# Modulation columns of a diffusion backbone: four blocks in one accumulation, transposes in place of selector matmuls

## The chip, the core and the metric

The kernel runs on one core of a Trainium2 chip. The metric is the device time of one execution in microseconds (us). In the profile, PE is TensorE's matmuls and PEld its weight loads, DVE is VectorE, ACT is ScalarE, POOL is GpSimd and SP is SyncE, which here issues DMAs. Each engine takes its instructions in the order in which they stand in the program, and waits for other engines by semaphores.

## What is computed

Two layers over a latent grid of 1024 positions and a context of 256, with a width of 1024: first windowed attention with 16 query heads and 4 key/value heads, then a bidirectional state-space scan. Before each mixer the normalised input is scaled and shifted, and what the mixer gives is multiplied by a gate. Scale, shift and gate come from two condition vectors, one for the latents and one for the context:

```python
def adaln(cond, w, b):
    mod = jax.nn.silu(cond) @ w + b
    return jnp.split(mod, 3, axis=-1)

for i in range(DEPTH):
    shift, scale, gate = adaln(c, w_ada[i], b_ada[i])
    shift_c, scale_c, gate_c = adaln(c_ctx, w_ada[i], b_ada[i])
    u = rms_normalize(h) * (1.0 + scale[:, None]) + shift[:, None]
    uc = rms_normalize(hc) * (1.0 + scale_c) + shift_c
    ...
    h = h + gate[:, None] * y
```

So each layer has a matrix w_ada of 1024 x 3072, by which two vectors are multiplied. The result for the layer is wanted with its 3072 values along the partitions, as 24 tiles of 128, and two columns (latents, context): the array mod.

## The kernel before

The activations lie transposed, features on partitions, in three token tiles: i = 0 and 1 (512 latents each) and i = 2 (256 context positions). Matmuls of the projections are done with operands split into a high and a low part: three fp32r matmuls for each of 8 slices of 128 features (lines L227 to L229, into PSUM tiles named pj), 24 matmuls for a projection of 128 outputs and one token tile. Weights are loaded by SP into tiles wr; ACT casts the high part (wh, L213), POOL or DVE subtracts the low part (wl, L215).

The stage of qkvg computes keys and values first. Then a loop over x = 0..7 computes queries for the token tiles 2 and 0 (q_step), and a second loop over x = 0..7 computes gates (g_step, tile 2 for all x, tile 0 for x from 4 on). Behind each of these projections, fill(m) takes m small steps (3, 3, 3, 2 in turn) off a list named ada. That list is the modulation work that isn't needed at once: of the 12 column blocks of 512 columns (6 for each layer), layer 0's blocks 0 to 3 are done at the start (ada0), and the eight blocks left, (0, 4), (0, 5) and (1, 0) to (1, 5), are fillers.

For a block, adaln_col makes nine steps. Steps k = 0..7 each load one slab of w_ada of 128 x 512 (256 KB) into a buffer of the rings wh or wl, four buffers each. After the fourth and the eighth load, four matmuls run. Each has a stationary operand of 32 columns (the condition vectors at feature slice k, in the first two of 32 columns, the rest zero) and the slab as the moving one, and writes 32 of the 128 PSUM partitions of the tile aps: a strip of TensorE's array for each of four values of k. So the sum over k lies spread over four strips when the block is done. The ninth step, fin, copies aps to SBUF (L189, tile qf), and modulation (L201) multiplies each of its four 128-column parts by a selector sel of 128 x 2 that adds the four strips up and brings the columns onto partitions; DVE adds the bias (L203), and adds 1 or halves where the block is a scale or a layer 0 gate (L205, L192).

The instructions of an engine are not in the order of the code. A scheduler orders them when the program is built, by dependencies, priorities and its own expectation of when things are ready. Behind the stage, the pools of the stage are closed; attention (att_front, att_back) then runs with the rest of the query and gate projections as its own fillers.

Of the kernel before, what the change touches and what calls it, by code (L numbers as in the profile page):

```python
# [9 lines left out]
F32 = mybir.dt.float32  # L10
# [3 lines left out]
ALU = mybir.AluOpType  # L14
# [3 lines left out]
P = 128  # L18
D = 1024
KT = D // P  # L20
# [85 lines left out]
class Kernel:  # L106
# [13 lines left out]
    def t(self, pool, shape, dt, tag, bufs=None):  # L120
        self.n += 1
        kw = {"bufs": bufs or BUFS.get(tag, 1)}
        return pool.tile(shape, dt, tag=tag, name=f"{tag}_{self.n}", **kw)
# [45 lines left out]
        self.bada = t(cp, [P, 2, 24], F32, "bada")  # L169
        nc.sync.dma_start(self.bada, self.a["bada"].rearrange("p (l t) -> p l t", l=2))  # L170

    def adaln_col(self, layer, n, pool, ps):

        nc, t = self.nc, self.t
        st = {}

        def step(k):
            if k == 0:
                st["ps"] = t(ps, [P, 512], F32, "aps", 2)
            raw = t(pool, [P, 4, P], F32, ("wh", "wl")[k // 4])  # L180
            nc.sync.dma_start(raw, self.a["w_ada"][layer, n, k].rearrange("p (a c) -> p a c", a=4))
            st[k] = raw
            if k % 4 == 3:
                for j in range(4):
                    nc.tensor.matmul(st["ps"][32 * j : 32 * j + 32], self.cs[:, k - 3 + j, :], st[k - 3 + j].rearrange("p a c -> p (a c)"), start=k == 3, stop=k == KT - 1)

        def fin():
            row = t(self.pq, [P, 512], F32, "qf")
            nc.scalar.copy(row, st["ps"])  # L189
            m = self.modulation(layer, n, row, ps)  # L190
            if n // 2 == 2 and layer == 0:
                nc.vector.tensor_scalar_mul(m, m, 0.5)  # L192

        return [lambda k=k: step(k) for k in range(KT)] + [fin]

    def modulation(self, layer, n, row, ps):

# [322 lines left out]
    def qkvg(self, p, wk, wvp):  # L520
        nc, t, a = self.nc, self.t, self.a
        ps = self.psA
        nc.gpsimd.dma_start(self.mask, a["mask"])
        nc.sync.dma_start(self.sink, a["sink"].broadcast_to([P, HEADS]))
        nc.vector.tensor_scalar_mul(self.nsink, self.sink, -1.0)
        v = self.v
        NB = (LAT + CTX) // P
        kh_d = [[t(self.dr, [P, n], F32, f"k{x}_{i}") for i, (_, n) in enumerate(TT)] for x in range(2)]

        wv = [self.load_w(a["wv"][q // 2, :, q % 2 * 512 : q % 2 * 512 + 512], 2, 256, pool=wvp, eng=nc.gpsimd) for q in range(4)]  # L530

        def kproj(x, i):
            s, n = TT[i]
            h, l = self.qk(p, self.proj_h(ps, wk[x], self.uH, self.uL, i), i)
            nc.vector.tensor_copy(self.kL[x][:, s : s + n], l)
            nc.sync.dma_start(kh_d[x][i], h.bitcast(F32))
            for e in range(2):
                for hf in range(2):
                    nc.gpsimd.dma_start(self.kHH[2 * x + e][hf * HD : (hf + 1) * HD, s : s + n], kh_d[x][i][e * HD : (e + 1) * HD, :])

        def vproj(b):
            i = 0 if b < 4 else (1 if b < 8 else 2)
            o = (b * P) - TT[i][0]
            pj = t(ps, [P, 512], F32, "pj")
            self.mm3(pj[:, :256], [(self.uH[i][:, k, o : o + P], self.uL[i][:, k, o : o + P],
                                    wv[k // 2][0][:, k % 2, :], wv[k // 2][1][:, k % 2, :]) for k in range(KT)])
            pv = pj[:, :256].rearrange("p (j d) -> p j d", j=KV)
            nc.scalar.copy(v[:, b, :, :HD], pv)
            nc.vector.tensor_sub(v[:, b, :, HD:], pv, v[:, b, :, :HD])  # L549

        for i, (s, n) in enumerate(TT):
            for x in range(2):
                kproj(x, i)
            if not VLAST:
                for b in range(s // P, (s + n) // P):
                    vproj(b)
        for b in range(NB if VLAST else 0):
            vproj(b)
        ada = []
        for layer, n in [(0, 4), (0, 5)] + [(1, n) for n in range(6)]:  # L560
            ada += self.adaln_col(layer, n, wvp, ps)

        def fill(m):
            for f in ada[:m]:
                f()
            del ada[:m]

        n = [3, 3, 3, 2]
        for x in range(8):
            w = self.load_halves(a["wq"][x])  # L570
            for i in (2, 0):
                self.q_step(p, w, x, i)
                fill(n[x % 2 * 2 + (i == 0)])
        for x in range(8):
            w = self.load_halves(a["wg"][x])
            for i in (2, 0) if x >= G0 else (2,):
                self.g_step(p, w, x, i)
                fill(n[x % 2 * 2 + (i == 0)])
        fill(len(ada))
# [972 lines left out]
```

## Time and profile before

| what | us |
|---|---|
| three runs: 1886.82, 1890.34, 1890.7; median | 1890.34 |
| span of the profiled execution, first to last instruction | 1886.0 |
| PE busy in it | 1790.8 (95%) |
| DVE busy | 1186.5 (63%) |
| ACT busy | 906.5 (48%) |
| POOL busy | 751.1 (40%) |

The profile is of one execution, of which only the span is given. The mean granted TensorE clock is 0.979 of full speed. The slices of the page show the rough shape; each digit is a busy share in tenths, for a fortieth (47 us) of the span:

```profile
PE   6779998899999899879999999999999999999997
PEclk9889999999999999989999999999999999999998
DMA  9338765653345456220111111111111111433552
```

The fillers lie in the fourth to sixth slice. A row of the timeline gives start, duration, engine, line, operation, output and inputs, shapes and how many records were merged; idle time before it and what ended it stand in brackets. An fp32 matmul of the fillers shows as two records (x8 is four strips), an fp32r matmul of the projections as one, an fp32 transpose as one. Consecutive matmuls overlap, so the distance from start to start is what one takes, not its duration.

### The profile page before, as it was taken

To read this page: it belongs to the slowest core of one execution; us is meant where nothing else is said; L and a number is where in the kernel's file an instruction comes from. 1 tells how busy PE (TensorE), PEld (TensorE's weight loads), DVE (VectorE), ACT (ScalarE), POOL (GpSimd) and SP (SyncE) were. 2 spreads that over 40 slices of the span, in tenths; PEclk is the share of its full clock that TensorE was granted. 3 is DMA by queue.
4 is the path that set the end of the run, shared out by engine and by line. 5 is a ranking of instruction groups with operands and counts; after the bars stand their busy time and mean duration, and the time that the engine had idled before them with its cause. 6 is when DMAs were issued, how large, how long until landed. Compare 5 with 4: busy or idle time off the path is not lost. (4 is left out here: it accounts for less than half of the span.)

```text
span 1886.0 us, 29647 instructions
## 1 busy us (share of the span) xinstructions
PE 1790.8 (95%) x10632; PEld 1543.2 (82%) x10632; DVE 1186.5 (63%) x2214; ACT 906.5 (48%) x1863; POOL 751.1 (40%) x1026
## 2 busy tenths in 40 slices
PE   6779998899999899879999999999999999999997
PEld 3678776788889787668898898989889898988887
DVE  4753425887777766584665757666575766754743
ACT  4522225677787765472353534434353543543532
POOL 2731105664456464302334352524335252442411
PEclk9889999999999999989999999999999999999998
DMA  9338765653345456220111111111111111433552
GB/s 358 111 79 251 233 209 132 143 124 95 96 118 135 112 137 198 87 55 23 49 36 44 44 36 44 36 44 36 43 47 33 44 39 41 138 119 100 176 162 68
DMA packets 147204, 192.10 MB, mean 102 GB/s; under 512 B 15313, under 2 KB 84817, under 8 KB 147057
## 3 DMA queue, kind: packets, MB, share of 16 engines
q1 hardware_dynamic: 112992, 171.56, 29.1%
q0 software_dynamic: 34064, 18.65, 5.6%
q8 instruction: 84, 1.38, 0.3%
q14 instruction: 64, 0.52, 0.1%
HBM read 154.54 MB, written 35.92 MB: 101 GB/s over the span
## 5 line engine op out<-in xcount | busy, mean ns | idle before, releaser
L227 PE MATMUL pj<-uH,wh 128*128 128x512 f32 (+1 forms) x712 | 258.8, 365 | 27.1 <-DVE v L549 9.5
L228 PE MATMUL pj<-uL,wh 128*128 128x512 f32 (+1 forms) x712 | 245.6, 345 | 1.5 <-DVE uL L441 1.2
L229 PE MATMUL pj<-uH,wl 128*128 128x512 f32 (+1 forms) x712 | 245.0, 344 | 1.3 <-POOL wl L215 1.3
L1066 POOL TENSOR_TENSOR xw<-xn,dtdec 128x256 f32<-128x256 f32 x144 | 106.4, 741 | 205.7 <-PE psD L1089 102.5
L227 PEld LDWEIGHTS pj<-uH,wh 128*128 128x128 f32 x712 | 136.9, 193 | 55.8 <-issue 19.1
L991 PE MATMUL pj<-uH,wh 128*128 128x512 f32 x512 | 171.7, 405 | 0.8 <-ACT xn L958 0.8
L991 PE MATMUL pj<-uH,wl 128*128 128x512 f32 x512 | 171.7, 404 | 0.0
L991 PE MATMUL pj<-uL,wh 128*128 128x512 f32 x512 | 168.7, 399 | 0.0
L215 POOL TENSOR_TENSOR wl<-wr,wh 128x512 fp32r<-128x512 f32 x96 | 125.7, 1313 | 97.9 <-ACT wh L213 97.2
L1016 PE MATMUL pj<-wh,uH 128*128 128x256 f32 x512 | 154.7, 302 | 0.0
L638 DVE TENSOR_TENSOR pl<-pt,ph 128x512 fp32r<-128x512 f32 x168 | 114.4, 688 | 63.5 <-ACT ph L637 62.8
L1016 PE MATMUL pj<-wh,uL 128*128 128x256 f32 x512 | 151.4, 296 | 0.0
L1016 PE MATMUL pj<-wl,uH 128*128 128x256 f32 x512 | 151.0, 295 | 0.0
L229 PEld LDWEIGHTS pj<-uH,wl 128*128 128x128 f32 x712 | 136.3, 192 | 17.7 <-POOL wl L215 1.7
L228 PEld LDWEIGHTS pj<-uL,wh 128*128 128x128 f32 x712 | 137.1, 193 | 15.7 <-DVE uL L441 3.6
L213 ACT CAST wh<-wr 128x512 fp32r<-128x512 f32 (+1 forms) x136 | 86.9, 644 | 124.7 <-PE pj L228 88.0
L1195 ACT ACTIVATE uT<-psX,nw 128x128 f32<-128x128 f32 x128 | 47.0, 367 | 189.8 <-PE psX L1194 188.6
L612 DVE CUSTOM_DVE_ANT_0 sm<-S,mask,nsink 128x640 f32<-128x640 f32 (+2 forms) x160 | 119.2, 772 | 23.2 <-PE S L609 11.9
L637 ACT CAST ph<-pt 128x512 fp32r<-128x512 f32 x168 | 97.3, 585 | 61.3 <-PE pt L633 55.6
L614 ACT ACTIVATE sm<-sm,nm 128x640 f32<-128x640 f32 (+2 forms) x160 | 118.6, 742 | 11.0 <-DVE nm L612 10.4
L1161 POOL TENSOR_TENSOR xs<-xn,sk 128x256 f32<-128x256 f32 x64 | 42.0, 656 | 184.7 <-DVE sk L1157 183.4
L991 PEld LDWEIGHTS pj<-uL,wh 128*128 128x128 f32 x512 | 95.6, 188 | 19.9
(332 smaller groups left out, 4994.8 us busy)
## 6 DMA issues: line engine op xcount, KB each, us to landing
wr<-w_x SPq DMA_DIRECT2D x32, 512.0 KB
wr<-wo SPq DMA_DIRECT2D x48, 256.0 KB
wr<-w_sk SPq DMA_DIRECT2D x24, 512.0 KB
wr<-wg SPq DMA_DIRECT2D x40, 256.0 KB
qs<-q POOLq DMA_DIRECT2D x40, 256.0 KB, 3.9
wada<-w_ada SPq DMA_DIRECT2D x16, 512.0 KB
wr<-wq SPq DMA_DIRECT2D x32, 256.0 KB
wl<-w_ada SPq DMA_DIRECT2D x32, 256.0 KB
```

The source lines that it names most:

```text
L213: nc.scalar.copy(h, raw)
L215: (eng or nc.vector).tensor_tensor(l, raw, h, op=ALU.subtract)
L227: self.nc.tensor.matmul(ps, lh, rh, start=first and i == 0, stop=False)
L228: self.nc.tensor.matmul(ps, lh, rl, start=False, stop=False)
L229: self.nc.tensor.matmul(ps, ll, rh, start=False, stop=last and i == n - 1)
L612: nc.vector.tensor_tensor_reduce(out=sm[:, :W], in0=Sv, in1=self.mask[:, m0 : m0 + W], scale=-SCALE, scalar=self.nsink[:, 4 * j + r : 4 * ...
L614: nc.scalar.activation(sm[:, :W], sm[:, :W], AF.Exp, bias=nm[:, r : r + 1], scale=-1.0, accum_out=sums[:, r : r + 1])
L637: nc.scalar.copy(ph, ptf)
L638: nc.vector.tensor_sub(pl, ptf, ph)
L991: nc.tensor.matmul(raw[:, 512 * i : 512 * i + 512], l[:, k, :], r[i][:, k, :], start=k + y == 0, stop=k == KT - 1 and y == 2)
L1016: nc.tensor.matmul(pj[:, c], l, r[:, k, :], start=c % 2 + q + k + y == 0, stop=c % 2 == 1 and q == 1 and k == 3 and y == 2)
L1066: nc.gpsimd.tensor_tensor(xw, X(st, c).rearrange("p (r h) -> p r h", r=R), self.dtdec[:, c, hd(d, g)].unsqueeze(2).broadcast_to([P, R, HP] ...
```

## The change

The eight blocks are taken four at a time. A step is now one load, for slice k and block q of four; after the fourth block's load, four matmuls run, one for each block, into that block's strip. All eight slices accumulate in the same tile, so that strip q holds the whole sum of block q. Two closings follow in place of eight: each copies the tile, transposes its four 128-column parts with the identity (L192 of the changed kernel), and DVE takes each block's two columns out of every part with the bias added (L196). The list of fillers has 66 steps in place of 72; fill takes as many at a time as before. The tags of the buffers alternate with k instead of changing after four slabs.

```diff
-    def adaln_col(self, layer, n, pool, ps):
+    def adaln_cols(self, blocks, pool, ps):
 
         nc, t = self.nc, self.t
         st = {}
 
-        def step(k):
-            if k == 0:
+        def step(k, q):
+            if k == q == 0:
                 st["ps"] = t(ps, [P, 512], F32, "aps", 2)
-            raw = t(pool, [P, 4, P], F32, ("wh", "wl")[k // 4])
-            nc.sync.dma_start(raw, self.a["w_ada"][layer, n, k].rearrange("p (a c) -> p a c", a=4))
-            st[k] = raw
-            if k % 4 == 3:
+            layer, n = blocks[q]
+            st[q] = t(pool, [P, 512], F32, ("wh", "wl")[k % 2])
+            nc.sync.dma_start(st[q], self.a["w_ada"][layer, n, k])
+            if q == 3:
                 for j in range(4):
-                    nc.tensor.matmul(st["ps"][32 * j : 32 * j + 32], self.cs[:, k - 3 + j, :], st[k - 3 + j].rearrange("p a c -> p (a c)"), start=k == 3, stop=k == KT - 1)
+                    nc.tensor.matmul(st["ps"][32 * j : 32 * j + 32], self.cs[:, k, :], st[j], start=k == 0, stop=k == KT - 1)
 
         def fin():
             row = t(self.pq, [P, 512], F32, "qf")
             nc.scalar.copy(row, st["ps"])
-            m = self.modulation(layer, n, row, ps)
-            if n // 2 == 2 and layer == 0:
-                nc.vector.tensor_scalar_mul(m, m, 0.5)
-
-        return [lambda k=k: step(k) for k in range(KT)] + [fin]
+            mt = t(ps, [P, 512], F32, "pt")
+            for j in range(4):
+                nc.tensor.transpose(mt[:, j * P : (j + 1) * P], row[:, j * P : (j + 1) * P], self.ident)
+            mv = mt.rearrange("p (j q c) -> p j q c", j=4, q=4)
+            for q, (layer, n) in enumerate(blocks):
+                m = self.mod[layer][:, n * 4 : n * 4 + 4, :]
+                nc.vector.tensor_tensor(m, mv[:, :, q, :2], self.bada[:, layer, n * 4 : n * 4 + 4].unsqueeze(2).broadcast_to([P, 4, 2]), op=ALU.add)
+                if n // 2 == 1:
+                    nc.vector.tensor_scalar_add(m, m, 1.0)
+                elif n // 2 == 2 and layer == 0:
+                    nc.vector.tensor_scalar_mul(m, m, 0.5)
+
+        return [lambda k=k, q=q: step(k, q) for k in range(KT) for q in range(4)] + [fin]
...
-        for layer, n in [(0, 4), (0, 5)] + [(1, n) for n in range(6)]:
-            ada += self.adaln_col(layer, n, wvp, ps)
+        for blocks in ([(0, 4), (0, 5), (1, 0), (1, 1)], [(1, n) for n in range(2, 6)]):
+            ada += self.adaln_cols(blocks, wvp, ps)
```

From L195 of before on, lines of the changed kernel have numbers that are 8 higher. Three places show what the scheduler makes of it. The first is on PE, a closing of before that stands within the first batch of the next block (L185 are strip matmuls, L201 the selector matmuls, L227 to L229 a projection):

```order
L229 MATMUL pj_1754<-uH_182_633,wl_1752 128x256
L185 MATMUL aps_1739<-wh_1740,cs_35_119 32x512
L201 MATMUL pt_1733<-sel_108,qf_1731 128x2 x4
L185 MATMUL aps_1739<-wh_1787,cs_35_119 32x512
L185 MATMUL aps_1739<-wh_1789,cs_35_119 32x512
L185 MATMUL aps_1739<-wh_1791,cs_35_119 32x512
L227 MATMUL pj_1797<-uH_94_243,wh_1744 128x512
```

This happens twice before; there are six other closings amid projection matmuls. Now there are two closings, both amid projection matmuls; the first of them (L192 are the transposes, L235 to L237 a projection):

```order
L235 MATMUL pj_1884<-uH_94_243,wh_1834 128x512
L192 MATMUL pt_1821<-ident_63,qf_1819 128x128 x4
L236 MATMUL pj_1884<-uL_95_244,wh_1834 128x512
L237 MATMUL pj_1884<-uH_94_243,wl_1836 128x512
L235 MATMUL pj_1884<-uH_94_243,wh_1834 128x512
```

No batch of four strips is cut by a closing any more. The second place is on PE too, the fifth batch of four strips, before:

```order
L229 MATMUL pj_1588<-uH_94_243,wl_1539 128x512
L185 MATMUL aps_1583<-wh_1584,cs_35_119 32x512
L185 MATMUL aps_1583<-wh_1586,cs_35_119 32x512
L185 MATMUL aps_1583<-wh_1627,cs_35_119 32x512
L185 MATMUL aps_1583<-wh_1629,cs_35_119 32x512
L227 MATMUL pj_1647<-uH_182_633,wh_1637 128x256
```

And now, one projection earlier (the dots stand for further matmuls of the same projection, six and four of them):

```order
L237 MATMUL pj_1533<-uH_182_633,wl_1531 128x256
L185 MATMUL aps_1263<-wh_1519,cs_35_119 32x512
L185 MATMUL aps_1263<-wh_1566,cs_35_119 32x512
L235 MATMUL pj_1576<-uH_94_243,wh_1523 128x512
...
L236 MATMUL pj_1576<-uL_95_244,wh_1523 128x512
L185 MATMUL aps_1263<-wh_1568,cs_35_119 32x512
L237 MATMUL pj_1576<-uH_94_243,wl_1525 128x512
...
L236 MATMUL pj_1576<-uL_95_244,wh_1529 128x512
L185 MATMUL aps_1263<-wh_1570,cs_35_119 32x512
```

The batch is spread over a projection in three pieces of two strips, one and one. The same happens to the thirteenth batch; the other fourteen stand in one piece. The third place is on ACT, in the opening of attention (sm are the exponentials of the softmax, ph casts of transposed probabilities, wh casts of weights, co a copy out of PSUM), before:

```order
L649 COPY co_2771<-pv_2704 64x512
L614 ACTIVATE sm_2789,sums_2785<-sm_2789,nm_2784 128x256
L614 ACTIVATE sm_2795,sums_2785<-sm_2795,nm_2784 128x256
L637 CAST ph_2823<-pt_2818 128x512
L637 CAST ph_2857<-pt_2852 128x512
L614 ACTIVATE sm_2801,sums_2785<-sm_2801,nm_2784 128x256
L614 ACTIVATE sm_2807,sums_2785<-sm_2807,nm_2784 128x256
L618 ACTIVATE es_2697<-es_2697 128x4
L213 CAST wh_2730<-wr_2728 128x512
L213 CAST wh_2736<-wr_2734 128x512
```

And now, from the same copy on:

```order
L657 COPY co_2723<-pv_2656 64x512
L626 ACTIVATE es_2649<-es_2649 128x4
L221 CAST wh_2682<-wr_2680 128x512
L221 CAST wh_2688<-wr_2686 128x512
L622 ACTIVATE sm_2741,sums_2737<-sm_2741,nm_2736 128x256
L622 ACTIVATE sm_2747,sums_2737<-sm_2747,nm_2736 128x256
L622 ACTIVATE sm_2753,sums_2737<-sm_2753,nm_2736 128x256
L645 CAST ph_2775<-pt_2770 128x512
L221 CAST wh_2817<-wr_2815 128x512
L221 CAST wh_2823<-wr_2821 128x512
L645 CAST ph_2809<-pt_2804 128x512
```

The weight casts stand ahead of exponentials and of casts that they followed. PE, DVE, POOL and SP have other sequences in these first units of attention as well; behind them the orders agree again, but for some twenty rows on PE where the second layer starts.

## The prediction

> **What bounds the kernel now.** The modulation work that the change touches runs in one stage, so the first view to read is the busy time by stretches: the projection stage (150 to 287 us), its handover to attention (287 to 299), the opening of attention (299 to 380) and the rest of attention. A row gives the stretch, its length, then busy time and count of PE, PEld, DVE, ACT and POOL, the granted clock, the DMA share and GB/s.
>
> ```profile
> 150.00:287.00 137.00, 137.00 (x842) 107.02 (x841) 50.60 (x101) 34.49 (x64) 15.39 (x12) 1.00 0.72 224
> 287.00:299.00 12.00, 5.00 (x28) 3.27 (x26) 4.88 (x19) 4.29 (x13) 3.69 (x8) 0.86 0.75 176
> 299.00:380.00 81.00, 73.67 (x391) 59.55 (x391) 61.41 (x156) 53.05 (x144) 58.59 (x82) 0.98 0.59 135
> 380.00:785.00 405.00, 390.13 (x2232) 329.19 (x2231) 288.86 (x593) 280.34 (x601) 220.50 (x298) 0.99 0.48 127
> ```
>
> PE is busy for all 137.00 us of the projection stage, at a granted clock of 1.00, while the other engines have at least 63% slack there. Whatever leaves PE in this stage therefore leaves the time. A busy PE need not be full, though: in this stage I count start to start, not by durations. The second view is who waited for whom on PE from 148 to 300 us (total, times, longest):
>
> ```profile
> PE pj L227 <- ACT wh L213: 5.3, 1, 5.3
> PE S L609 <- DVE nm L612: 1.6, 2, 1.4
> ```
>
> These are all its listed waits, and both fall after 287 us. No w_ada load stops PE now. From 380 us on PE is busy 390.13 of 405 us, so an earlier start there should last to the end.
>
> **The change, part by part.** The stage holds 64 strip matmuls of 32x512 (two records each) and, in the eight closings, 32 selector matmuls:
>
> ```profile
> 150.00:287.00 137.00, 19.12 (x128) 2.78 (x128) 4.70 (x8) 1.00 0.72 224
> 150.00:287.00 137.00, 7.79 (x64) 8.08 (x64) 1.00 0.72 224
> ```
>
> The first row is the tile aps, the second line L201. The 64 strip matmuls stay: 8 per column block before, 32 per four blocks now. What matters is in how many pieces they run. A piece is a run of strip matmuls with no other instruction between them. The timeline of PE around one whole piece of four strips:
>
> ```profile
> 159.03 0.28 PE L228 MATMUL pj<-uL,wh 128*128 128x256 f32 x1
> 159.15 0.28 PE L229 MATMUL pj<-uH,wl 128*128 128x256 f32 x1
> 159.36 1.06 PE L185 MATMUL aps<-wl,cs 128*32 128x512 f32 x8
> 160.36 0.50 PE L227 MATMUL pj<-uH,wh 128*128 128x512 f32 x1
> 160.69 0.39 PE L228 MATMUL pj<-uL,wh 128*128 128x512 f32 x1
> 160.92 0.40 PE L229 MATMUL pj<-uH,wl 128*128 128x512 f32 x1
> ```
>
> Projection matmuls start 0.12 us apart at 256 columns and 0.23 at 512. Without the piece, the matmul that starts at 160.69 would have started 0.12 + 0.23 after 159.15, at 159.50. So **a piece of four costs 1.19 us**. Now one closing, four selector matmuls that stand alone:
>
> ```profile
> 165.27 0.39 PE L227 MATMUL pj<-uH,wh 128*128 128x512 f32 x1
> 165.50 0.95 PE L201 MATMUL pt<-sel,qf 128*128 128x2 f32 x8
> 166.30 0.49 PE L228 MATMUL pj<-uL,wh 128*128 128x512 f32 x1
> 166.63 0.40 PE L229 MATMUL pj<-uH,wl 128*128 128x512 f32 x1
> ```
>
> From 165.27 to 166.63 are 1.36 us; less two spacings of 0.23 that is **0.90 us for a closing**. In two places of before, a closing stands inside a piece (the order shows it after the first strip, and later before the last):
>
> ```profile
> 200.29 0.28 PE L229 MATMUL pj<-uH,wl 128*128 128x256 f32 x1
> 200.50 1.04 PE L185 MATMUL aps<-wh,cs 128*32 128x512 f32 x2
> 201.48 1.05 PE L201 MATMUL pt<-sel,qf 128*128 128x2 f32 x8
> 202.46 1.06 PE L185 MATMUL aps<-wh,cs 128*32 128x512 f32 x6
> 203.45 0.50 PE L227 MATMUL pj<-uH,wh 128*128 128x512 f32 x1
> 203.79 0.39 PE L228 MATMUL pj<-uL,wh 128*128 128x512 f32 x1
> ```
>
> From 200.29 to 203.79 are 3.50 us; less 0.12 and 0.23 that is 3.15, which is 1.06 more than 1.19 + 0.90. The reader is to see why: one strip alone holds PE for 0.98 us (200.50 to 201.48), three for 0.99 (202.46 to 203.45). Strips run side by side, so **a piece costs the same with one strip as with four**, and each cut costs another piece.
>
> Before, then: 16 pieces x 1.19 + 8 closings x 0.90 + 2 cuts x 1.06 = 19.04 + 7.20 + 2.12 = 28.36 us.
>
> After: the closings shrink to two, of four fp32 transposes each. The trace has that same operation in attention:
>
> ```profile
> 323.50 0.40 PE L640 MATMUL pv<-pl,v 128*128 128x512 f32 x1
> 323.74 0.60 PE L633 MATMUL pt<-ident,sm 128*128 128x128 f32 x4
> 324.10 0.48 PE L227 MATMUL pj<-uH,wh 128*128 128x512 f32 x1
> 324.42 0.39 PE L228 MATMUL pj<-uL,wh 128*128 128x512 f32 x1
> ```
>
> From 323.50 to 324.42 are 0.92 us; less two spacings of 0.23 this leaves 0.46 for four; two closings cost 0.92. The Trainium skill has a rule against this part: "TensorE: Matmul & The Clock Gate", section "Part 4: PE-mode transpose", gives a 128x128 transpose about 275 ns inside a kernel. By it, as an estimate, eight cost 2.2 us and the whole change would gain 2.4 us. The row above has the same operation back to back at 0.115 us each, so the measurement decides.
>
> Both closings stand amid projection matmuls in the new order and cut no piece, so the 2.12 us go. But the new order has cuts of its own: two of the 16 batches of four strips stand as two strips, then one, then one, with projection matmuls between. That is 14 whole pieces and 6 short ones. Of a short piece between projections no row exists. It cannot cost less than nothing if the strip hides entirely; the nearest rows, 0.98 us for one strip plus the 0.09 and 0.10 us lost on either side of a whole piece, give 1.17. I take 1.19 and keep zero as the other end. After: 20 pieces x 1.19 + 0.92 = 24.72 us. **Sum: 24.72 - 28.36 = -3.6 us.**
>
> The six steps that vanish from the list of fillers (72 become 66) move every later batch forward against the projections, the last one by three projections, so loads must land sooner. The cut batches show where the order expects them late. The first cut:
>
> ```profile
> 170.89 0.80 SPq L181 DMA_DIRECT2D wh<-w_ada  x2
> 177.18 1.02 SPq L181 DMA_DIRECT2D wh<-w_ada  x2
> ...
> 180.47 0.40 PE L227 MATMUL pj<-uH,wh 128*128 128x512 f32 x1
> ...
> qs<-q POOLq DMA_DIRECT2D x40, 256.0 KB, 3.9
> ```
>
> SP's order is unchanged up to there, so the four loads of this batch are issued where these rows stand, the last two at about 177.2 and 177.7, each about 0.9 us sooner by the closing that is gone. PE reaches the batch at about 179.6 (the 512-column projection behind it started at 180.47 before). Then come 1.19 for the first piece and 8 x 0.23 to the next, so it wants the third load at 182.6 and the fourth at 185.2: 6.3 and 8.4 us after issue. A transfer of this size, issued by POOL, lands in 3.9 us. I cost the loads at nothing; if they took twice 3.9 us, PE would stand 1.5 us here.
>
> ACT makes two copies out of PSUM instead of eight and DVE still adds eight times; both have slack (50.60 and 34.49 of 137 us), so this is worth nothing. SP still issues 64 loads of 256 KB, sometimes ahead of weight loads that stood before them; those weights are used 20 us and more later, and PE has no wait on them now.
>
> At the handover the chain is the same in both orders: last projection, its gate row to DRAM, cosine and sine tables into the space freed, then the first attention weights:
>
> ```profile
> 291.47 2.33 SPq L220 DMA_DIRECT2D wr<-wq  x2
> ...
> 298.17 0.62 ACT L213 CAST wh<-wr 128x512 fp32r<-128x512 f32 x1 [5.88 <-DMA wr<-wq]
> ...
> 298.84 0.79 PE L227 MATMUL pj<-uH,wh 128*128 128x512 f32 x1 [5.27 <-ACT wh L213]
> ```
>
> It hangs on the last projection, so it moves with it. The first q loads of attention wait for strip pieces and come earlier, but PE never waited for them; worth nothing.
>
> **The rivals.** *The opening of attention takes the gain back.* The new order has other sequences on all engines in the first units. On ACT, four weight casts now stand ahead of exponentials and of two casts (ph) that PE waits for. Where they ran before:
>
> ```profile
> 302.23 0.59 ACT L649 COPY co<-pv 64x512 f32<-64x512 f32 x1 [0.46 <-PE pv L640]
> ...
> 305.88 0.61 ACT L213 CAST wh<-wr 128x512 fp32r<-128x512 f32 x1
> 306.70 0.62 ACT L213 CAST wh<-wr 128x512 fp32r<-128x512 f32 x1 [0.20 <-PE pj L228]
> ...
> 311.62 0.62 ACT L213 CAST wh<-wr 128x512 fp32r<-128x512 f32 x1
> ...
> 314.48 0.62 ACT L213 CAST wh<-wr 128x512 fp32r<-128x512 f32 x1 [0.75 <-ACT sm L614]
> ```
>
> After the copy co ACT would stand from 302.8 to 305.88, 3.1 us, and from the first ph (about 309.3: 307.3 plus four operations of some 0.5) to 315.1, less two casts, 4.6 us. If PE paid all 7.7, the time would be 1890.3 - 3.6 + 7.7 = 1894.4, slower; it decides from 3.6 us paid. Against it: PE has two projections of 24 matmuls, 11 us at 0.23, to run meanwhile, and these casts' loads arrive no later than before.
>
> *The short pieces hide.* If single strips slip between projections for nothing, the four cuts (4.76 us) cost nothing and the gain is 8.4: 1881.9. For it speaks only that no row shows them; the 0.98 us of a lone strip speaks against.
>
> *Loads come late at the new places.* With up to 1.5 us at each cut and some at the moved last batch, 3 us, the time is 1889.7, no change. For it: a DMA share of 0.72 in the stage.
>
> *The change doesn't do what it says.* If the strips of four blocks did not run side by side, 16 batches would take 3 x 0.98 us more each, 47 us, 1934. Before already used four strips in one piece, so this is remote. Or the gain vanishes at the handover, held by something that doesn't move: 1890.3.
>
> **How the numbers follow.** The profiled execution spans 1886.0 us; the three runs gave 1886.82 to 1890.7, so its span lies 4.3 below their median, and the sum, small against that, is set off the median: 1890.3 - 3.6 = 1886.7. About 0.2% (3.8 us) is what a measurement of this kernel can tell from no change, and the forecast lies at that edge. Chances: forecast 0.58, with its own range of 1884 to 1889.5, since the opening of attention has 7.3 us of idle PE between 299 and 380 that a new order can shift by a few us (0.30 of it faster, 0.28 within the bound); short pieces hidden 0.12 (faster); loads late 0.13 (same); opening of attention 0.12 (0.09 slower, 0.03 same); gain held at the handover 0.03 (same); strips not side by side 0.02 (slower). Together faster 0.42, same 0.47, slower 0.11. The range runs from the hidden pieces to most of the opening's price: 1881 to 1893.
>
> **What would show it right or wrong.** In the profile after, line L192 should hold eight transposes at 0.46 us for four, L185 still 128 records in 20 pieces, and the six short ones should hold PE about 1 us each. The last projection should end near 283 us instead of 287, with no PE wait on a w_ada load before it. Then the idle PE from there to the end of attention's opening should be that of before. It is wrong if a short piece costs much less than 1 us, if PE waits at the cut batches, or if the first 90 us of attention hold several us more or less idle PE.

## The result, and the profile after

| | before | after |
|---|---|---|
| median of 19 runs each | 1891.68 us | 1887.68 us |
| lowest and highest | 1886.82, 1894.95 | 1882.48, 1891.27 |
| ratio after to before | | 0.9976 (95%: 0.9967 to 0.9985) |
| span of the profiled execution | 1886.0 us | 1880.8 us |
| PE busy in it | 1790.8 us | 1786.4 us |

The changed kernel is faster by 0.24%, some 4 us, where 3.6 us were forecast. The busy time by stretches of the changed kernel, in the columns of the prediction's first fence (projection stage, handover, opening of attention, rest of attention):

```profile
150.00:283.00 133.00, 132.18 (x781) 99.86 (x779) 50.84 (x102) 31.46 (x58) 15.39 (x12) 1.00 0.71 228
283.00:296.00 13.00, 9.71 (x38) 6.67 (x39) 7.15 (x28) 7.87 (x24) 6.65 (x11) 0.78 1.15 202
296.00:376.00 80.00, 72.94 (x386) 59.10 (x385) 59.01 (x148) 49.59 (x132) 56.67 (x80) 0.97 0.55 131
376.00:781.00 405.00, 389.08 (x2235) 328.45 (x2234) 289.85 (x592) 279.88 (x600) 219.22 (x297) 0.99 0.47 127
```

(Nothing rests on the DMA share of 1.15, which is printed as the view has it.) The stage is still PE without a gap: up to the first score matmul at 281.55 it is busy all the time, and the 0.82 us of idle time in the first row lie behind that. To measure the stage well it needs two marks that both programs have: the last value matmul (pj from wh and uL) and the first score matmul S of attention. On PE's timeline of before:

```profile
146.74 0.28 PE L229 MATMUL pj<-wh,uL 128*128 128x256 f32 x1
...
286.85 0.40 PE L609 MATMUL S<-kHH,qs 128*128 128x256 f32 x2
```

And of after:

```profile
145.00 0.28 PE L237 MATMUL pj<-wh,uL 128*128 128x256 f32 x1
...
281.55 0.40 PE L617 MATMUL S<-kHH,qs 128*128 128x256 f32 x2
```

**The stage lasted 140.11 us before and 136.55 us after: 3.56 us less, by a sum that said 3.64** (28.36 - 24.72). That the mark at its start lies 1.74 us earlier as well need not be the work of the change: over the twelve executions profiled for this study it lies anywhere from 144.5 to 149.8 us, for the same program too, and what follows the opening of attention lasts 1510.3 to 1517.1 us. These parts make single times differ by 5 us and more; the stage repeats to 0.07 us. So from here on stages are compared, and times only where there are many.

PE's waits of after between 148 and 300 us (total, times, longest) show no load of w_ada, and the first one is the handover's, 1.9 where before had 5.3:

```profile
PE pj L235 <- ACT wh L221: 1.9, 1, 1.9
PE S L617 <- DVE nm L620: 1.6, 2, 1.3
PE S L617 <- issue: 0.7, 1, 0.7
```

The new forms on PE's timeline of after, first the batch that the order cut in three, then a closing:

```profile
177.70 0.28 PE L237 MATMUL pj<-uH,wl 128*128 128x256 f32 x1
177.91 1.05 PE L185 MATMUL aps<-wh,cs 128*32 128x512 f32 x4
178.89 0.50 PE L235 MATMUL pj<-uH,wh 128*128 128x512 f32 x1
179.23 0.39 PE L236 MATMUL pj<-uL,wh 128*128 128x512 f32 x1
...
180.62 0.39 PE L236 MATMUL pj<-uL,wh 128*128 128x512 f32 x1
180.93 1.04 PE L185 MATMUL aps<-wh,cs 128*32 128x512 f32 x2
181.91 0.50 PE L237 MATMUL pj<-uH,wl 128*128 128x512 f32 x1
182.25 0.39 PE L235 MATMUL pj<-uH,wh 128*128 128x512 f32 x1
...
210.04 0.39 PE L235 MATMUL pj<-uH,wh 128*128 128x512 f32 x1
210.27 0.60 PE L192 MATMUL pt<-ident,qf 128*128 128x128 f32 x4
210.62 0.48 PE L236 MATMUL pj<-uL,wh 128*128 128x512 f32 x1
210.94 0.40 PE L237 MATMUL pj<-uH,wl 128*128 128x512 f32 x1
```

Two strips: 179.23 - 177.70 = 1.53, less the spacings 0.12 and 0.23, is 1.18 us. One strip: 182.25 - 180.62 = 1.63, less 0.46, is 1.17. A closing: 0.90 - 0.46 = 0.44.

### The profile page after: what moved, and what is told of

Its sections match the earlier page's. It is cut to its first block, busy times and chain, and to the rows that moved or that the text cites. A ratio compares the mean times of both kernels' runs of the same rounds, so it can differ in the third digit from the quotient of the medians.

```text
span 1880.8 us, 29512 instructions
## 1 busy us (share of the span) xinstructions
PE 1786.4 (95%) x10576; PEld 1535.8 (82%) x10576; DVE 1185.9 (63%) x2214; ACT 903.0 (48%) x1857; POOL 751.4 (40%) x1026
## 5 line engine op out<-in xcount | busy, mean ns | idle before, releaser
L235 PE MATMUL pj<-uH,wh 128*128 128x512 f32 (+1 forms) x712 | 259.1, 366 | 19.5 <-DVE v L557 9.5
L237 PE MATMUL pj<-uH,wl 128*128 128x512 f32 (+1 forms) x712 | 244.8, 344 | 1.6 <-POOL wl L223 1.6
L235 PEld LDWEIGHTS pj<-uH,wh 128*128 128x128 f32 x712 | 137.1, 193 | 50.3 <-issue 17.7
L237 PEld LDWEIGHTS pj<-uH,wl 128*128 128x128 f32 x712 | 136.1, 191 | 19.8 <-POOL wl L223 2.0
```

The costliest lines, as they stand in the source:

```text
L235: self.nc.tensor.matmul(ps, lh, rh, start=first and i == 0, stop=False)
L237: self.nc.tensor.matmul(ps, ll, rh, start=False, stop=last and i == n - 1)
```

## The experiments

The lengths below come from PE's timeline and from ACT's copies co, one for each unit of attention. The stage is as above; the handover runs from the first score matmul to the first projection inside attention; the opening, from the same mark to the ninth copy co, contains the handover. Pieces are counted in the program's order on PE. The handover ends where the order has its first projection, and orders differ in what they have ahead of it, before and after by one value matmul only; so elsewhere in this column equal lengths need not have the same cause.

| kernel | pieces | stage | handover | opening | time, us |
|---|---|---|---|---|---|
| before | 16 + 2 cuts by closings | 140.11 | 11.99 | 88.84 | 1891.68 |
| before again (e5) | the same | 140.11 | 11.64 | 89.30 | 1894.43, one run |
| after | 20 | 136.55 | 8.55 | 88.50 | 1887.68 |
| after again (e1) | 20 | 136.62 | 8.39 | 88.26 | 1885.39, one run |
| transposes only (e3) | as before | 136.66 | 11.95 | 89.01 | 1888.59 |
| selector in the group (e4) | 20 | 137.42 | 11.36 | 86.51 | 1886.46, one run |
| whole batches (e2) | 16 | 131.70 | 9.00 | 86.83 | 1878.18 |
| whole batches again (e8) | 16 | 131.70 | 9.26 | 87.91 | 1879.20 |
| 25 pieces (e7) | 25 | 142.34 | 10.91 | 83.91 | 1886.92, one run |
| 34 pieces (e6) | 34 | 153.09 | 11.40 | 85.88 | 1896.72, one run |
| transposes x 20 (e9) | 20 | 153.07 | 11.49 | 85.53 | 1897.90, one run |
| matmuls x 10 (e10) | 20 | 153.48 | 11.39 | 85.75 | 1898.11, one run |

Beside e1 to e4 the median of before was 1892.15 us, beside e5 to e8 1891.53; a single run of it beside e9 and e10 took 1891.02.

### Chance or order: both programs once more (e1, e5)

> The changed kernel once more, nothing edited. The stage length is counted from the start of the last value matmul to the start of the first score matmul: 140.11 us before, 136.55 after. If the stage's gain is a matter of the order on PE alone, it is 136.5 to 136.6 again. What lies outside (1.7 us at the start, 3.4 us at the handover from projections to attention, and their loss in the units behind it) is measured a second time: if the handover's gain belongs to this order, the first attention projection again starts about 8.6 us after the first score matmul (12.0 before); if it was chance, it lies anywhere between 8.5 and 12.

> The kernel before, unchanged, for a second trace. If stage and handover belong to the order, the stage (from the last value matmul to the first score matmul) is 140.1 us again within 0.1, and the handover (first score matmul to first attention projection) 12.0 within 0.3, while the start of the stage may lie 2 us away from 146.74. If the 3.4 us between the two handovers were chance, this handover could be as short as 9.

Stage and handover came back in both programs (136.62 and 8.39, 140.11 and 11.64), while the start of the stage moved by about 3 us in each (147.84 and 149.79). The handover of e5 lies 0.36 us below 12.0, where 0.3 had been allowed, but far from the 9 of the rival. So the 3.5 us of the stage and the 3.3 us of the handover belong to the two orders.

### Whole batches (e2, e8)

```diff
-        n = [3, 3, 3, 2]
+        n = [2, 4, 2, 4]
```

In the changed kernel, fill takes two and four steps in turn, twelve for four projections where it was eleven. The scheduler then leaves all 16 batches of four strips whole, and one of the two closings stands beside a piece.

> The changed kernel with fill counts of 2, 4, 2, 4 in place of 3, 3, 3, 2; in its order all 16 batches stand in one piece. Theory (a piece costs 1.19 us whether it holds one strip or four): 16 x 1.19 + 0.92 = 19.96 in place of 24.72 us, so the stage length is 136.55 - 4.76 = 131.8 and the whole about 4.8 us less than the changed kernel, 1883, ratio to before 0.995. Rival (only the number of strip matmuls counts, short pieces hide between projections): stage length 136.5 as now, ratio 0.9976.

> The kernel of e2 (16 whole pieces) again, for a second trace and comparison. Stage 131.7 within 0.1, opening to the ninth copy co 86.8 within 0.4; by stage and opening together 10.4 us below before (8.4 + 2.0), ratio about 0.9945. If e2's ratio of 0.9929 was no accident, again below 0.994.

The stage is 131.70 us twice (149.69 to 281.39 in e2), 4.9 below the changed kernel for four pieces fewer; the ratios to before are 0.9929 (0.991 to 0.9948) and 0.9935 (0.9915 to 0.9956). This version beats both kernels. Stage and opening account for 8.41 and 1.70 us (means of two traces each), 10.1 us; the two ratios say 13.4 and 12.3, with bounds that both take in 10.1. Two expectations missed: the ratio of e2 lies below 0.995, its upper bound of 0.9948 only just, and the opening of e8 is 87.91 us, where 86.8 within 0.4 was expected. Where the 2 to 3 us come from that the ratios have beyond 10.1 is not shown.

### Transposes without the grouping (e3)

```diff
-        for j in range(4):
-            nc.tensor.matmul(mt[:, 2 * j : 2 * j + 2], row[:, j * P : (j + 1) * P], self.sel, start=True, stop=True)
...
+            for j in range(4):
+                nc.tensor.transpose(mt[:, j * P : (j + 1) * P], row[:, j * P : (j + 1) * P], self.ident)
+            mv = self.t(self.pq, [P, 4, 2], F32, "mv")
+            nc.vector.tensor_reduce(mv, mt.rearrange("p (j s r) -> p j r s", j=4, s=4)[:, :, 0:2], axis=mybir.AxisListType.X, op=ALU.add)
```

The kernel before, one block at a time and eight closings; the closings of the fillers transpose, and DVE adds the four strips.

> The kernel before, with four transposes and a DVE reduction over the four strips in each of the eight closings in place of the selector matmuls; its order on PE is that of before. Theory (0.46 us for four transposes, 0.90 for four selector matmuls): 8 x 0.44 = 3.5 us less, stage length 136.6. Rival (a transpose costs 0.275 us inside a kernel): 8 x 1.1 = 8.8 us for the closings in place of 7.2, stage length 141.7.

The stage is 136.66 us (147.06 to 283.72), 3.45 below before, and the ratio 0.9974 (0.9957 to 0.9991): **as much as the whole change brings**, without the common accumulation. The grouping saves six more closings (6 x 0.46) and the two cuts (2.12), 4.88 us, and pays four extra pieces (4 x 1.18 = 4.72) for them. In e2 the pieces are not paid. That "its order on PE is that of before" holds for the stage only: at the handover four records of score matmuls and one of a value matmul that before has later stand ahead of the first projection, and PE's long wait, 3.39 us, lies ahead of a value matmul. So the handover of 11.95 us is as long as before's for another reason; SP asks for the cosine table 0.51 us behind the gate row there, as in after.

### The grouping with the selector's kind of closing (e4)

```diff
-                nc.tensor.transpose(mt[:, j * P : (j + 1) * P], row[:, j * P : (j + 1) * P], self.ident)
+                nc.tensor.matmul(mt[:, 8 * j : 8 * j + 8], row[:, j * P : (j + 1) * P], self.ident.rearrange("p (q r) -> p q r", r=32)[:, :, 0:2], start=True, stop=True)
...
```

> The changed kernel with selector matmuls (128x8, fp32) in place of the transposes in its two closings; its order in the stage is the same. Theory: 2 x 0.90 in place of 2 x 0.46, stage length 136.55 + 0.9 = 137.4. Were the transposes the main part of the gain, it would go back towards 140.1.

The stage is 137.42 us, 0.83 above the changed kernel (136.59, the mean of two); two closings at 0.90 instead of 0.46 make 0.88. The price of a closing holds in both directions.

### More pieces, the same matmuls (e6, e7)

e6 takes four steps behind every projection, e7 issues each strip in the step of its load:

```diff
-        n = [3, 3, 3, 2]
+        n = [4, 4, 4, 4]
```

```diff
-            if q == 3:
-                for j in range(4):
-                    nc.tensor.matmul(st["ps"][32 * j : 32 * j + 32], self.cs[:, k, :], st[j], start=k == 0, stop=k == KT - 1)
+            nc.tensor.matmul(st["ps"][32 * q : 32 * q + 32], self.cs[:, k, :], st[q], start=k == 0, stop=k == KT - 1)
```

> The changed kernel with four filler steps behind each projection. The same 64 strip matmuls and 8 transposes; the scheduler places them in 34 pieces, nearly all of the 18 extra ones single strips, in place of 20. Theory (a piece costs 1.18 whatever its number of strips): stage 111.8 + 34 x 1.18 + 0.92 = 152.9 us, 16.3 above the changed kernel, and a time about 1900. Rival 1 (single strips between projections hide at least in part): below 148. Rival 2 (the loads, asked for faster, come late): above 155, with PE waits on w_ada tiles.

> The changed kernel with each strip matmul issued in the step of its load instead of four behind the fourth load. The same matmuls in 25 pieces of one to three strips, one of them beside a closing. Theory: stage 111.8 + 25 x 1.18 + 0.92 = 142.2, less 0.1 to 0.2 where the closing stands at a piece: 142.1 us, 2.0 above the kernel before though it has all that the change brings besides. Rival (the cost goes by strips, not by pieces): 136.6 as the changed kernel.

The stages are 153.09 and 142.34 us. One of the single strips of e6, on PE's timeline:

```profile
152.64 0.39 PE L235 MATMUL pj<-uH,wh 128*128 128x512 f32 x1
152.96 1.04 PE L185 MATMUL aps<-wh,cs 128*32 128x512 f32 x2
153.93 0.50 PE L236 MATMUL pj<-uL,wh 128*128 128x512 f32 x1
154.27 0.39 PE L237 MATMUL pj<-uH,wl 128*128 128x512 f32 x1
```

It costs 1.63 - 0.46 = 1.17 us again. Neither kernel has a PE wait on a w_ada tile in the stage, though e6 asks for 16 loads in four projections where the changed kernel asks for 11. From 20 to 34 pieces the stage grew by 16.5 us, 1.18 for each; the rivals of both runs fall.

### Do transposes keep the clock up? (e9, e10)

```diff
-                nc.tensor.transpose(mt[:, j * P : (j + 1) * P], row[:, j * P : (j + 1) * P], self.ident)
+                for r in range(20):
+                    nc.tensor.transpose(mt[:, j * P : (j + 1) * P], row[:, j * P : (j + 1) * P], self.ident)
```

e10 has matmul with the identity in place of transpose, ten times over. What raised the question stands in the next section: the clock halved in a place where PE had run little but transposes.

> The changed kernel with each of the eight transposes of the closings made twenty times over (the same result written again), so that two stretches of 80 transposes stand on PE without a gap. At 0.115 us each a stretch is 9.2 us and the stage 136.6 + 2 x 8.7 = 154.1 us. The question is what made the clock halve at 362 us in the changed kernel, where PE was never idle for more than 1.7 us but had run only transposes from 356.4 to 360.97. Theory 1 (transposes do not count as activity for the granted clock): within each stretch the clock falls to 0.50 after some 3 to 7 us and comes back only some 3 to 7 us behind it, as it does after idle time; the stage is then 5 to 15 us longer than 154.1. Theory 2 (the sum of the idle bits did it): clock 1.00 all through, stage 154.1.

> The control to e9: in place of the eight transposes the same products with the identity as plain fp32 matmuls of 128 x 128, ten times each, so that two stretches of 40 stand on PE without a gap. By four selector matmuls in 0.90 us one costs about 0.23 us, a stretch 9.2 us, the stage about 154. Both theories: clock 1.00 all through. If the clock falls here as well, the length of the stretch or the copy before it is at work, not the kind of operation.

One of the two stretches on the timeline of e9:

```profile
211.10 0.39 PE L236 MATMUL pj<-uH,wh 128*128 128x512 f32 x1
211.33 8.89 PE L193 MATMUL pt<-ident,qf 128*128 128x128 f32 x80
219.98 0.48 PE L237 MATMUL pj<-uL,wh 128*128 128x512 f32 x1
220.30 0.40 PE L238 MATMUL pj<-uH,wl 128*128 128x512 f32 x1
```

And the windows around it (stretch, length, PE busy and count, granted clock, DMA share, GB/s):

```profile
211.00:220.00 9.00, 9.00 (x85) 1.00 0.69 222
220.00:230.00 10.00, 10.00 (x66) 1.00 0.28 84
```

The clock stays at 1.00 in the stretch and behind it, and in the control. Theory 1 falls for transposes that follow one another closely; that the idle bits did it is what is left, and no run varied them. Eighty transposes took 8.65 us, 0.108 each; 152 more of them make 16.4, and the stage grew by 16.5; the 154.1 expected was 1.0 too much because it counted 0.115 for each. Forty plain fp32 matmuls of 128 columns took 8.84 us (209.94 to 218.78 in e10), 0.22 each, twice a transpose; that stage, 153.48 us, came out 0.5 below the 154 expected.

## Why the prediction was right, point by point

**The bound.** That PE sets the length of this stage held in every kernel: the stages of e2 to e8, from 131.7 to 153.1 us, came out within 0.25 us of the sums of PE's work on record above; those of e9 and e10 came out 1.0 and 0.5 us below theirs.

**The price of a piece** (1.19, the same for one strip as for four) was the step with no row behind it for short pieces. They cost 1.17 and 1.18, and e2, e6 and e7 show it by dose. "The short pieces hide" was wrong altogether.

**The closings** (0.90 before, 0.46 after) held: 0.44 in after, e3 by eight of them and e4 by two. By the price that the Trainium skill gives, in "TensorE: Matmul & The Clock Gate", section "Part 4: PE-mode transpose", about 275 ns for a bf16 transpose inside a kernel, the stage would have gained an estimated 2.4 us. The trace does not agree with it for these fp32 transposes: four of them cost 0.44 us in after.

**The loads** at nothing: right, with no PE wait on them at the new places, nor in e6.

**The sum** of the stage, -3.6, measured -3.56. The make-up is less kind to the change than the sum shows, though: by e3 the transposes alone bring it, and the grouping gains and loses 4.8 us within itself.

**The handover** was the step that was wrong. The prediction says of its chain that "it hangs on the last projection, so it moves with it". It got 3.3 us shorter besides (11.82 to 8.47, means of two traces). On SP's timeline of before, the cosine table's load stands idle behind the gate row sg:

```profile
288.46 0.33 SPq L512 DMA_DIRECT2D sg<-qf  x1
290.61 0.34 SPq L480 DMA_DIRECT2D cos<-cos  x1
```

SP's waits name what it waits for: until the gate row has landed.

```profile
SPq L480 <- DMA sg<-qf: 1.7, 1, 1.7
```

In after, SP does not wait there. The weights behind the tables are asked for 1.4 us after the gate row instead of 3.0 (291.47 in before, a row of the prediction), and the first projection follows (picked from the timeline of three engines):

```profile
283.09 0.33 SPq L520 DMA_DIRECT2D sg<-qf  x1
283.60 0.35 SPq L488 DMA_DIRECT2D cos<-cos  x1
...
284.49 0.90 SPq L228 DMA_DIRECT2D wr<-wq  x2
...
289.43 0.62 ACT L221 CAST wh<-wr 128x512 fp32r<-128x512 f32 x1 [2.25 <-DMA wr<-wq]
...
290.10 0.61 PE L235 MATMUL pj<-uH,wh 128*128 128x512 f32 x1 [1.90 <-ACT wh L221]
```

The 2.15 and 0.51 us between these two issues are the same in e5 and e1, and so the weights are asked for 1.6 us sooner in both: half of the 3.3 us. The other half lies between the request for the weights and their cast: 6.70 us in before (291.47 to 298.17) and 4.94 in after, 6.35 and 4.78 in e5 and e1. In before POOL's first load of queries (qs, 289.97) is asked for ahead of the weights, in after 0.12 us behind them (284.61); whether that is why they land sooner was not tried. Which earlier allocation in the pools makes the one program wait and not the other was not tried.

**The opening of attention** gave most of those 3.3 us back, though not by the mechanism of the rival. Its rows for before and for after, from the first score matmul to the ninth copy co (only PE's busy time, count and clock are used):

```profile
286.85:375.69 88.84, 74.75 (x394) 59.95 (x393) 62.78 (x167) 54.47 (x151) 59.35 (x85) 0.96 0.62 143
```

```profile
281.55:370.05 88.50, 77.56 (x394) 61.79 (x393) 61.63 (x167) 54.58 (x151) 58.76 (x85) 0.94 0.64 143
```

The same 394 records: idle time fell by 3.15 us (14.09 to 10.94), and the busy time grew by 2.81. Part of that lies at the handover itself: the clock reads 0.50 for 6.8 us there in both (from 295.6 in before, from 290.3 in after), but PE worked for 3.59 us of it in before and for 6.18 in after. The larger part sits between the eighth and the ninth copy co. Before:

```profile
363.10:375.69 12.59, 9.90 (x62) 1.00 0.49 113
```

After, that interval and then two stretches inside it:

```profile
354.86:370.05 15.19, 11.93 (x62) 0.89 0.37 95
356.40:362.00 5.60, 2.33 (x13) 1.00 0.75 175
362.00:365.40 3.40, 3.40 (x12) 0.50 0.31 101
```

The interval is 2.60 us longer (in e1 and e5 too: 15.19 against 12.60): 0.57 of it is idle PE, 2.03 are the same 62 records taking longer, because the clock halves behind the gaps for 3.40 us. The gaps are four waits in a row:

```profile
358.10 0.44 PE L654 MATMUL pt<-ident,rs 128*128 128x128 f32 x2 [1.70 <-POOL rs L630]
358.38 0.60 PE L641 MATMUL pt<-ident,sm 128*128 128x128 f32 x4
359.63 0.66 PE L641 MATMUL pt<-ident,sm 128*128 128x128 f32 x4 [0.66 <-DVE sgt L655]
360.97 0.50 PE L647 MATMUL pv<-ph,v 128*128 128x512 f32 x1 [0.68 <-ACT ph L645]
361.70 0.54 PE L648 MATMUL pv<-pl,v 128*128 128x512 f32 x1 [0.23 <-DVE pl L646]
```

The moved casts were not what PE waited for in bulk (ph 1.7 us in after's opening, 1.6 in before's), so the rival's 7.7 us never appeared. Why PE waits for rs, sgt, ph and pl just there in the new order was not traced. On balance the opening is 0.7 us shorter (89.07 to 88.38, means of two traces). With the stage's 3.5 that is 4.2 us, against 4.0 between the medians.

**How much was luck.** The mechanism and the size of the stage's gain were right. That the total came within 0.4 us of the forecast was in part luck: outside the stage the handover got 3.3 us shorter and the rest of the opening 2.7 us longer, each nearly as much as the whole gain, and the prediction had both at nothing. It had named several us more or less idle PE in the first 90 us of attention as a sign of being wrong, and there were 3.15 us less.

## What to carry to other kernels

Count such small matmuls by pieces: a run of strips side by side costs what one strip costs, 0.98 us and some 0.1 us on either side, so a layout that packs them loses its worth as the scheduler deals them out in more pieces (e6, e7), and one number in the pacing of the fillers (e2) was worth more than the algebra. Divide a change into its parts before praising the whole: here the transposes alone had all of the stage's gain. And measure a stage between two marks that both programs have; it repeated to 0.07 us where whole times spread over 8.

## What the runs showed of the hardware

The granted clock can halve without one gap as long as the slow stretch that follows. Read in windows of 0.2 us, it falls to 0.50 at three places of the two openings: at the handover from 295.6 to 302.4 in before and from 290.3 to 297.2 in after, and from 362.0 to 365.4 in after. These stretches last 6.8, 6.8 and 3.4 us, in the second traces too. In before the clock fell 2.0 us after PE's last matmul ahead of the long wait had ended (298.84 - 5.27 = 293.57); in after's opening it fell with no gap above 1.70 us. In the 3.4 us ahead of the three falls PE was busy for 1.32, 1.51 and 1.84 us. Yet in before, gaps in the same unit, the longest of 1.47 us, left it at 1.00:

```profile
365.60:369.30 3.70, 1.01 (x5) 1.00 0.88 179
```

So partly idle time can be enough, and the busy time of such a stretch does not by itself tell when.

The Trainium skill, "TensorE: Matmul & The Clock Gate", section "Part 1: The HAM clock gate", has two states, half and full, set by windows of about 3.4 us in which PE is idle or busy. The half clock and the stretches of 3.4 us and twice 3.4 us agree; that a window must be idle does not describe the three places, unless the activity in it counted as too little. The same page of the Trainium skill, section "Part 4: PE-mode transpose", says that the full clock doesn't engage for transposes, which don't count as PE activity in the same way; that would have explained 356.40 to 362.00. The 80 fp32 transposes of e9 ran 8.65 us at 1.00, so here they count; what share of idle time makes the clock fall stays open.

The opening's length was 83.9 to 89.3 us for the same computation in nine programs, whose edits lie elsewhere, while two traces of one program lay 0.2 to 1.1 us apart; the shortest belongs to e7, whose stage is 2.2 us longer than that of before. Its time of 1886.92 us, one run, is still below before's median. Such a shift can be as large as the change itself.
